# Out-projection weights split two tiles ahead, and eight low parts handed from VectorE to GpSimd, in a one-core decoder layer

## The chip, the cores and the metric

The kernel runs on one core of one Trainium2 chip. The metric is device time of one execution in microseconds; it is taken as the median over several executions. The profile is one further execution, recorded instruction by instruction.

## The reference, cut to what matters

One decoder layer over 1024 positions with width 1024 and a hidden width of 4096, all in float32:

```
h = x + concat[ sliding-window heads(RMSNorm(x)) | forgetting heads(RMSNorm(x)) ] @ W_o
y = h + relu( RMSNorm(h) @ W_u )**2 @ W_d
```

Eight heads use a banded softmax with sinks, eight use a causal softmax with a learned decay. The change touches the stretch in which `W_o` is multiplied, `h` is formed, and the factors for `W_u` are prepared.

## The kernel before, in words

Everything is kept with the features on the 128 partitions and the positions along the row. TensorE works on pairs of reduced-precision numbers: `split` (L73 to L80) casts a float32 tile to its high part on one engine, and then subtracts the high part from the tile on another engine, which gives the low part. Each product is three matmuls: high by high, high by low, low by high. A matmul of the line `mm` (L73) has 128x512 outputs in most stages.

**Attention.** The eight forgetting heads run two at a time. For each block of queries ScalarE makes the exponentials (`sb`, L689), VectorE scales them (L698), TensorE transposes them (`tpb`, L725), ScalarE casts the transposed tile (`pth`, L393), VectorE takes its low part (`ptl`, L394), and TensorE multiplies it with the values (`pvb`). The result of a head pair leaves by ScalarE and VectorE as `mtb` and `mix`, goes through a normalisation (`mixr`, `mixn`, `mixs`) out to a scratch tensor in memory `mixs_d` and comes back as the tile `mix6` (L850). In the gaps of these heads TensorE is given products of the out-projection.

**Out-projection.** The output has eight tiles `dt` of 128 features. `out_first` multiplies the first half of the contraction for all eight tiles and parks the sums, added to `x`, in the scratch tensor `part_d`. The second half is done by three functions. `out_weights(dt, 4)` loads 256 KB of `W_o` (`wor`, L857, two buffers), casts its high part on ScalarE (L77) and subtracts its low part on GpSimd (L80) into a tile `wos`, in the slots `w0` and `w1` by turns. `out_products` issues 24 matmuls. `out_finish` loads the parked sum (`h`, L956), adds the products on VectorE (L958), writes `h` to the scratch tensor `h_d` (L959), and makes the seven tiles `bh1` to `bh7` and their low parts `bl1` to `bl7` that the next stage multiplies: two or three are gained copies of `h`, made by `h_split` (L947 on ScalarE, L948 on VectorE), the others are sums `ts` (L965, L977), split by `sum_splits`. The tiles `dt` are finished in the order 0, 4, 1, 5, 2, 6, 3, 7. A pair (t, t + 4) fills the fourth `t` of every `bh` and `bl`; `ts` has one buffer, so that the sums of `t + 1` wait until all splits of `t` have read it.

Tiles 0 and 4 are begun inside the attention (`ahead_of`); the loop over 1, 5, 2, 6, 3, 7 makes weights, products and finish of one tile after the other.

**Up.** Seven products per column tile `j` of `W_u`, in the order 1, 2, 3, 6, 7, 5, 4, replace eight. `up(j)` builds sums of weights (`wus`, L1018, L1021), splits each weight tile `wu` (ScalarE casts, the low part is VectorE's for 2, 6, 5 and GpSimd's for the others), and issues 12 matmuls `pu` for each. The `wu` tiles rotate through the slots `w0` to `w6`, which the tiles `h` and `wos` had. Of `t` = 3, `bh5`, `bl5`, `bh4` and `bl4` are made after the product 2 of `j` = 0.

**What sets the order.** The engines run their instructions strictly in the order in which a scheduler wrote them down when the program was built. It works from the code's order, the data dependencies and its own costs; `issue_after` adds a dependency that only holds something back in that order. All loads and stores go through SyncE's queue, which is in order as well: a transfer that has to wait for a buffer holds up those behind it. GpSimd's and VectorE's work lies in their own queues in the same way.

Of the kernel before, what the change touches and what calls it, by code (L numbers as in the profile page):

```python
# [8 lines left out]
F32 = mybir.dt.float32  # L9
F32R = mybir.dt.float32r  # L10
BF16 = mybir.dt.bfloat16
AF = mybir.ActivationFunctionType
ALU = mybir.AluOpType
# [3 lines left out]
P = 128  # L17
# [38 lines left out]
def hybrid_layer(  # L56
# [13 lines left out]
    nc = tc.nc  # L70

    def mm(out, lhsT, rhs, start, stop):
        return nc.tensor.matmul(out, lhsT, rhs, start=start, stop=stop)  # L73

    def split(hi, lo, src, hi_eng, lo_eng):
        if hi_eng is nc.scalar:
            hi_eng.copy(hi, src)  # L77
        else:
            hi_eng.tensor_copy(hi, src)
        lo_eng.tensor_tensor(out=lo, in0=src, in1=hi.bitcast(F32), op=ALU.subtract)  # L80

    def rsqrt(pool, out, t, shape, tag):
        r0 = pool.tile(shape, F32, tag=tag + "r0", name="r0")
# [14 lines left out]
        out=ident, in_=ident, pattern=[[-1, P]], compare_op=ALU.not_equal,  # L98
# [17 lines left out]
    for i in range(2):  # L116
        nc.vector.tensor_tensor(
            out=gqk[:, i : i + 1], in0=vec[:, 2 * i : 2 * i + 1],
            in1=vec[:, 2 * i + 1 : 2 * i + 2], op=ALU.mult,
# [24 lines left out]
    def slot(tag, name, shape, dt=F32, pool=None):  # L144
        pool = o[pool or ("zw" if tag[0] == "w" else "zl")]
        return pool.tile([P] + shape, dt, tag=tag, name=name, bufs=1)
# [7 lines left out]
    def x_part(j, k, rows):  # L154

        c, r0 = divmod(rows.start, 512)
        return X[c][k // 2][:, j, k % 2, r0 : r0 + rows.stop - rows.start]
# [11 lines left out]
        out=maskd, in_=maskd, pattern=[[-1, P]], compare_op=ALU.is_ge,  # L169
# [6 lines left out]
    def w_tiles(n):  # L176


        w = wp.tile([P, 2 * WL], F32R, tag="w", name="w", bufs=8)
        wr = wp.tile([P, WN], F32, tag="wr", name="wr", bufs=3)  # L180
        lo = 384 if n == 384 else 400
        return wr[:, :n], w[:, :n], w[:, lo : lo + n]
# [10 lines left out]
    for k in range(KT):  # L193
        xr = ap2.tile([P, S], F32, tag="s", name="xr", bufs=NS)
        wr, wh, wl = w_tiles(384)
        if k == 0:
            nc.sync.dma_start(wr, w_a0[:, k, :])
            nc.scalar.preload_act_table_set("natural_log_exp_and_others")
        nc.sync.dma_start(xr[:, halves[0]], xT[k * P : (k + 1) * P, halves[0]])
        if k:  # L200
            nc.sync.dma_start(wr, w_a0[:, k, :])
        nc.sync.dma_start(xr[:, halves[1]], xT[k * P : (k + 1) * P, halves[1]])
        split(wh, wl, wr, nc.vector, nc.gpsimd if k else nc.vector)
        for cs in halves:
            hi, lo = (x_part(j, k, cs) for j in range(2))
            nc.scalar.activation(hi, xr[:, cs], AF.Copy, scale=ga[:, k : k + 1])
            last_x = nc.vector.scalar_tensor_tensor(  # L207
                out=lo, in0=xr[:, cs], scalar=ga[:, k : k + 1],
                in1=hi.bitcast(F32), op0=ALU.mult, op1=ALU.subtract,
            )  # L210
        passes = ((0, wh), (0, wl), (1, wh))
        order = (
            [(t, j) for j in range(3) for t in range(NT)] if k == 0
            else [(t, j) for t in (range(NT) if k < KT - 1 else LAST) for j in range(3)]
        )
        for t, j in order:
            part_, w_ = passes[j]
            mm(
                qps[t][:, :384], x_part(part_, k, slice(t * P, (t + 1) * P)), w_,
                k == 0 and j == 0, k == KT - 1 and j == 2,  # L220
            )
# [180 lines left out]
    for t in range(NT):  # L402
# [4 lines left out]
        out=rt, in0=rt, scalar1=1.0 / D, scalar2=EPS, op0=ALU.mult, op1=ALU.add  # L407
# [6 lines left out]
    for t in range(0, NT, 4):  # L414
# [8 lines left out]
        out=dist, in_=dist, pattern=[[-1, 256]], compare_op=ALU.is_ge, fill=BIG,  # L423
# [3 lines left out]
        out=dist, in_=dist, pattern=[[1, 256]], compare_op=ALU.is_ge, fill=BIG,  # L427
# [8 lines left out]
    for pattern, base, sign in (  # L436
# [5 lines left out]
            out=before, in_=before, pattern=pattern, compare_op=ALU.is_ge, fill=0.0,  # L442
# [407 lines left out]
        nc.sync.dma_start(mixt[e].bitcast(F32), mixs_d[e].rearrange("c p s -> p c s"))  # L850

    nout = [0]

    def out_weights(dt, e0):
        i = nout[0] = nout[0] + 1
        wr = o["zw"].tile([P, 4, P], F32, tag="wor", name="wor", bufs=2)
        nc.sync.dma_start(wr, w_o[dt][:, e0 : e0 + 4, :])  # L857
        w = slot(f"w{i % 2}", "wos", [2, 4, P], F32R)
        split(w[:, 0], w[:, 1], wr, nc.scalar, nc.gpsimd)
        return w[:, 0], w[:, 1]  # L860

    def out_products(ps, w, es):
        wh, wl = w
        for e in es:
            j = e % 4
            for c in range(2):
                cs = slice(c * 512, (c + 1) * 512)
                mm(ps[c], wh[:, j, :], mh[e][:, cs], j == 0, False)
                mm(ps[c], wh[:, j, :], ml[e][:, cs], False, False)
            for c in range(2):  # L870
                cs = slice(c * 512, (c + 1) * 512)
                mm(ps[c], wl[:, j, :], mh[e][:, cs], False, j == 3)

    def first_banks():
        return [o["pm0"].tile([P, 512], F32, tag=f"m{c}", name=f"po{c}") for c in range(2)]

    def out_first(dt):
        xt = slot(f"w{2 + dt % 2}", "xt", [S])
        nc.sync.dma_start(xt, xT[dt * P : (dt + 1) * P, :])
        w = out_weights(dt, 0)  # L880
        ps = first_banks()
        with paced():
            out_products(ps, w, range(4))
        t = slot("w4", "pc", [S])
        for c in range(2):
            cs = slice(c * 512, (c + 1) * 512)
            nc.scalar.copy(t[:, cs], ps[c])
            nc.gpsimd.tensor_tensor(out=xt[:, cs], in0=xt[:, cs], in1=t[:, cs], op=ALU.add)
        nc.sync.dma_start(part_d[dt], xt)
# [17 lines left out]
    for dt in (0, 4):  # L907
        ps = first_banks() if dt == 0 else [
            pa.tile([P, 512], F32, tag="sc", name=f"po{c}", bufs=2) for c in range(2)
        ]  # L910
        ahead_of.append((dt, ps, out_weights(dt, 4)))
# [25 lines left out]
    bh, bl = {}, {}  # L937
# [2 lines left out]
        bl[n] = slot(f"c{2 * i + 1}", f"bl{n}", [4, 512], F32R, "zr")  # L940
    rr = o["zr"].tile([P, S], F32, name="rr")
    left, right = slice(0, 512), slice(512, 1024)
    part = {}

    def h_split(n, t, src, gain):
        hi, lo = bh[n][:, t, :], bl[n][:, t, :]
# [5 lines left out]
    def out_finish(dt, ps):  # L952
        t, gain = dt % 4, gm[:, dt : dt + 1]
        h = slot(f"w{2 + dt // 4}", "h", [S]) if dt < 7 else rr
        with tc.issue_after(part["load"].ins) if dt == 7 else nullcontext():
            part["load"] = nc.sync.dma_start(h, part_d[dt])  # L956
        for c, cs in enumerate((left, right)):
            nc.vector.tensor_tensor(out=h[:, cs], in0=ps[c], in1=h[:, cs], op=ALU.add)  # L958
        nc.sync.dma_start(h_d[dt], h)  # L959
        if dt < 4:  # L960
            h_split(1, t, h[:, left], gain)
            ts = part["t"] = slot("m4", "ts", [4, 512])
            b12 = part["b12"] = slot("w4", "b12", [512])
            nc.scalar.activation(b12, h[:, right], AF.Copy, scale=gain)
            nc.vector.scalar_tensor_tensor(  # L965
                out=ts[:, 0], in0=h[:, left], scalar=gain, in1=b12, op0=ALU.mult, op1=ALU.subtract
            )
            return
        ts, b12 = part["t"], part["b12"]
        h_split(2, t, h[:, left], gain)  # L970
        h_split(3, t, h[:, right], gain)
        for i, q, other, op in (
            (1, right, ts[:, 0], ALU.add),
            (2, right, b12, ALU.subtract),
            (3, left, ts[:, 1], ALU.subtract),
        ):
            nc.vector.scalar_tensor_tensor(  # L977
                out=ts[:, i], in0=h[:, q], scalar=gain, in1=other, op0=ALU.mult, op1=op
            )
        part["rest"] = lambda: sum_splits(ts, t, ((0, 5), (3, 4)))  # L980
        sum_splits(ts, t, ((1, 6), (2, 7)))
        if t < 3:
            part.pop("rest")()

    def sum_splits(ts, t, which):
        for i, n in which:
            split(bh[n][:, t], bl[n][:, t], ts[:, i], nc.scalar, nc.vector)

    for dt, ps, w in ahead_of:
        out_finish(dt, ps)  # L990
    pda.close()
# [5 lines left out]
    def up_load(j):  # L997
        raws[j] = slot(f"r{j % 2}" if j else "m3", "wur", [2, KT, P])
        for i in range(2):
            up_loads[j] = nc.sync.dma_start(raws[j][:, i], w_u[j + i * NJ])  # L1000

    for dt in (1, 5, 2, 6, 3, 7):
        w = out_weights(dt, 4)
        ps = [bank(f"po{c}") for c in range(2)]
        out_products(ps, w, range(4, 8))
        out_finish(dt, ps)
        if dt == 2:
            with tc.issue_after(part["load"].ins):
                up_load(0)
# [267 lines left out]
    for i in range(len(STEPS)):  # L1277
        down(i)
        if STEPS[i][0] == len(PHASES) - 1 and late:
            name, dt, cs = late.pop(0)  # L1280
# [63 lines left out]
```

## Time and profile before

| | us |
|---|---|
| median of 3 executions | 1093.83 (1093.57 to 1095.04) |
| the profiled execution, by its own time | 1092.15 |
| its span | 1090.4 |
| TensorE busy in the span | 1078.7 (99%) |
| VectorE busy | 777.7 (71%) |
| ScalarE busy | 569.9 (52%) |
| GpSimd busy | 362.5 (33%) |

Times inside the profile run from the span's start. The attention's last heads run until about 436 us; the out-projection's last six tiles run on TensorE from 440.5 to 473.3; the first up products follow. A row of the timeline is: start, duration, engine, line, operation, output and inputs, shapes, how many in a row, and in brackets how long the engine had been idle and which instruction ended the wait. The durations of ScalarE's rows with x2 are of both together. SPq is SyncE's queue of transfers; the row of a transfer's issue says nothing of its landing, which the view of transfers gives.

### The profile page before, as it was taken

What the parts mean: (1) busy time and instruction counts of PE and PEld (TensorE: products, weight loads), DVE (VectorE), ACT (ScalarE), POOL (GpSimd) and SP (SyncE); (2) the same over time, 40 slices, a digit from 0 to 9 for tenths busy, and PEclk for the clock granted to TensorE, in tenths of its full rate; (3) what the DMA queues carried; (4) which work ended last, traced back from release to release, by engine and by line L of the source; (5) the groups of instructions that cost most, each with busy time, mean ns of one, the idle gap of its engine ahead of it and who ended that gap; (6) DMA issues with size and microseconds to landing.
All of it is one profiled execution on the core that took longest, in us unless ns stands there. A gap on an engine that the chain in (4) does not pass through costs nothing.

```text
span 1090.4 us, 15689 instructions
## 1 busy us (share of the span) xinstructions
PE 1078.7 (99%) x5557; PEld 933.5 (86%) x5557; DVE 777.7 (71%) x1327; ACT 569.9 (52%) x1013; POOL 362.5 (33%) x352
## 2 busy tenths in 40 slices
PE   9999999999999999999999999999999999999998
PEld 8999999999997888778888888888888888888886
DVE  7377677767765676998686869867675876674395
ACT  5558588666766756554545444353633433333331
POOL 5672523435434634333222232322222222231100
PEclk9999999999999999999999999999999999999999
DMA  9401212335656565663545543443998886665523
GB/s 308 141 27 48 72 37 61 115 87 154 209 192 221 167 223 174 212 231 126 198 179 179 189 153 135 149 170 145 333 390 311 299 289 227 241 228 181 174 87 116
DMA packets 96079, 195.69 MB, mean 179 GB/s; under 512 B 7376, under 2 KB 19584, under 8 KB 96000
## 3 DMA queue, kind: packets, MB, share of 16 engines
q1 hardware_dynamic: 95856, 194.66, 51.4%
q8 instruction: 44, 0.72, 0.3%
q14 instruction: 35, 0.29, 0.1%
q10 hardware_dynamic: 144, 0.02, 0.0%
HBM read 141.61 MB, written 53.04 MB: 179 GB/s over the span
## 4 chain that ended last, share of the span: by engine, by line
PE 82%; DMA 6%; DVE 6%; issue 2%; ACT 2%; POOL 1%; SPq 0%; ACTq 0%; POOLq 0%; DVEq 0%
PE pu L73 28%; PE pd L73 28%; PE ps L73 10%; PE po L73 5%; PE spb L73 3%; PE pvb L73 2%; PE tpb L725 2%; PE sp L73 1%; PE pv L73 1%; DMA wr<-in_w_b_dram 1%; DMA xq<-in_x_dram 1%; PE tpa L554 1%; DMA xr<-in_xT_dram 1%; DMA mixs_d<-mixn 1%; DVE x L207 1%
## 5 line engine op out<-in xcount | busy, mean ns | idle before, releaser
L73 PE MATMUL pd<-hx,wx 128*128 128x512 f32 (+1 forms) x1350 | 304.9, 388 | 0.0
L73 PEld LDWEIGHTS pd<-hx,wx 128*128 128x128 f32 x1350 | 252.7, 188 | 52.2
L73 PE MATMUL pu<-bh,wu 128*128 128x512 f32 x896 | 276.6, 390 | 1.0 <-ACT bh L947 1.0
L73 PE MATMUL ps<-w,x 128*128 128x384 f32 (+1 forms) x960 | 199.0, 345 | 0.4 <-DVE z L451 0.3
L73 PEld LDWEIGHTS pu<-bh,wu 128*128 128x128 f32 x896 | 168.1, 188 | 36.4 <-ACT bh L947 1.4
L73 PE MATMUL pu<-bl,wu 128*128 128x512 f32 x448 | 174.0, 389 | 0.0
L73 PEld LDWEIGHTS ps<-w,x 128*128 128x128 f32 x960 | 165.2, 189 | 3.7 <-DVE z L451 0.6
L77 ACT CAST hx<-hr 128x1024 fp32r<-128x1024 f32 x56 | 59.1, 1055 | 176.2 <-PE pd L73 171.2
L80 POOL TENSOR_TENSOR wx<-wda,wx 128x1024 fp32r<-128x1024 f32 x24 | 64.5, 2687 | 196.4 <-ACT wx L77 196.4
L80 DVE TENSOR_TENSOR hx<-hr,hx 128x1024 fp32r<-128x1024 f32 x56 | 72.2, 1297 | 71.0 <-ACT hx L77 71.0
L73 PEld LDWEIGHTS pu<-bl,wu 128*128 128x128 f32 x448 | 84.1, 188 | 17.7 <-issue 0.2
L73 PE MATMUL po<-mix,wos 128*128 128x512 f32 x384 | 94.8, 396 | 1.0 <-ACT wos L77 1.0
L73 PEld LDWEIGHTS po<-mix,wos 128*128 128x128 f32 x384 | 70.5, 188 | 15.5 <-ACT wos L77 1.5
L80 POOL TENSOR_TENSOR wu<-wus,wu 128x512 fp32r<-128x512 f32 x32 | 45.6, 1426 | 113.0 <-ACT wu L77 113.0
L80 POOL TENSOR_TENSOR wu<-wur,wu 128x512 fp32r<-128x512 f32 x32 | 44.2, 1380 | 102.5 <-ACT wu L77 102.5
L1018 DVE TENSOR_TENSOR ht<-hb 128x512 f32<-128x512 f32 x32 | 21.8, 723 | 62.8 <-ACT hb L1073 62.8
L394 DVE TENSOR_TENSOR ptl<-tpb,pth 128x512 fp32r<-128x512 f32 (+1 forms) x80 | 49.5, 631 | 21.9 <-ACT pth L393 18.9
L80 POOL TENSOR_TENSOR w<-wr,w 128x384 fp32r<-128x384 f32 (+1 forms) x47 | 51.5, 1106 | 40.1 <-ACT w L77 29.4
L77 ACT CAST wu<-wus 128x512 fp32r<-128x512 f32 x64 | 38.0, 618 | 48.3 <-PE pu L73 39.9
L77 ACT CAST wx<-wda 128x1024 fp32r<-128x1024 f32 x56 | 58.5, 1049 | 6.6 <-DMA wda<-in_w_d_dram 6.6
L689 ACT ACTIVATE sb<-sb,nmb 128x128 f32<-128x128 f32 (+3 forms) x64 | 49.8, 779 | 22.7 <-DVE nmb L683 22.6
L1072 ACT ACTIVATE hb<-hb 128x2048 f32<-128x2048 f32 x16 | 30.7, 1917 | 48.0 <-DVE hb L1021 47.9
(210 smaller groups left out, 1839.3 us busy)
## 6 DMA issues: line engine op xcount, KB each, us to landing
wda<-in_w_d_dram SPq DMA_DIRECT2D x34, 1024.0 KB, 9.2
hr<-hid_d SPq DMA_DIRECT2D x56, 512.0 KB, 5.7
wur<-in_w_u_dram SPq DMA_DIRECT2D x32, 512.0 KB, 4.3
hid_d<-ht SPq DMA_DIRECT2D x16, 1024.0 KB, 4.5
hid_d<-hb SPq DMA_DIRECT2D x16, 768.0 KB, 3.6
mix<-mixs_d SPq DMA_DIRECT2D x7, 1024.0 KB, 5.8
wr<-in_w_b_dram SPq DMA_DIRECT2D x32, 192.0 KB, 2.5
xr<-in_xT_dram SPq DMA_DIRECT2D x16, 256.0 KB, 5.0
```

Source lines behind the costliest of these rows:

```text
L73: return nc.tensor.matmul(out, lhsT, rhs, start=start, stop=stop)
L77: hi_eng.copy(hi, src)
L80: lo_eng.tensor_tensor(out=lo, in0=src, in1=hi.bitcast(F32), op=ALU.subtract)
L207: last_x = nc.vector.scalar_tensor_tensor(out=lo, in0=xr[:, cs], scalar=ga[:, k : k + 1], in1=hi.bitcast(F32), op0=ALU.mult, op1=ALU.subtract,
L394: nc.vector.tensor_tensor(out=lo[:, cols], in0=pt[:, cols], in1=hi[:, cols].bitcast(F32), op=ALU.subtract)
L554: nc.tensor.transpose(tp[:, hh * P : (hh + 1) * P], pts[hh // 2][:, hh % 2, c0 : c0 + P], ident)
L689: nc.scalar.activation(pr[:, :nk], pr[:, :nk], AF.Exp, scale=-1.0, bias=nm[:, c : c + 1], accum_out=dn_b[p % 2][:, h, i : i + 1] if p < 3 ...
L725: nc.tensor.transpose(tp[:, c0 : c0 + P], probs[qi][:, kb * P : (kb + 1) * P], ident)
L1018: eng.tensor_tensor(out=out, in0=a, in1=b, op=ALU.subtract)
L1072: nc.scalar.activation(b, b, AF.Relu)
```

## The change: what it does

Three things.

1. The weights of tiles 1 and 5 are made before the finishes of tiles 0 and 4 are written down. These two weight tiles go to the slots `w6` and `w5`.
2. In the loop, the weights of the tile two places on are made after a tile's products and before its finish.
3. The low parts `bl5` and `bl4` (eight instructions, two for each `t`) are GpSimd's and no longer VectorE's. `issue_after` places them behind the low part of the weights that were made last before.

```diff
@@ split
-        lo_eng.tensor_tensor(out=lo, in0=src, in1=hi.bitcast(F32), op=ALU.subtract)
+        return lo_eng.tensor_tensor(out=lo, in0=src, in1=hi.bitcast(F32), op=ALU.subtract)
@@ out_weights
-        w = slot(f"w{i % 2}", "wos", [2, 4, P], F32R)
-        split(w[:, 0], w[:, 1], wr, nc.scalar, nc.gpsimd)
+        w = slot(f"w{i % 2 + (5 if i in (11, 12) else 0)}", "wos", [2, 4, P], F32R)
+        part["weights"] = split(w[:, 0], w[:, 1], wr, nc.scalar, nc.gpsimd)
@@ sum_splits
         for i, n in which:
-            split(bh[n][:, t], bl[n][:, t], ts[:, i], nc.scalar, nc.vector)
+            last = n in (5, 4)
+            with tc.issue_after(part["weights"].ins) if last else nullcontext():
+                split(
+                    bh[n][:, t], bl[n][:, t], ts[:, i], nc.scalar,
+                    nc.gpsimd if last else nc.vector,
+                )
+    rest = (1, 5, 2, 6, 3, 7)
+    ws = [out_weights(dt, 4) for dt in rest[:2]]
     for dt, ps, w in ahead_of:
         out_finish(dt, ps)
...
-    for dt in (1, 5, 2, 6, 3, 7):
-        w = out_weights(dt, 4)
+    for i, dt in enumerate(rest):
         ps = [bank(f"po{c}") for c in range(2)]
-        out_products(ps, w, range(4, 8))
+        out_products(ps, ws[i], range(4, 8))
+        if i + 2 < len(rest):
+            ws.append(out_weights(rest[i + 2], 4))
         out_finish(dt, ps)
```

What this makes of the engines' orders is shown at two places. The numbers behind the names tell tiles apart. The first place is ScalarE's order in the last part of the attention, from the cast of `mixn_5210` on, which is the row of 412.78 us in the timeline before. `wos_5606` belongs to tile 4. Before:

```order
L77 CAST mixn_5210<-mixr_5209 128x512
L689 ACTIVATE sb_5462,dnb_5464<-sb_5462,nmb_5463 128x256
L887 COPY pc_5445<-po0_5419 128x512
L887 COPY pc_5445<-po1_5420 128x512
L77 CAST wos_5606<-wor_5604 128x512
L393 CAST pth_5391<-tpb_5387 128x384
L393 CAST pth_5478<-tpb_5473 128x512
L689 ACTIVATE sb_5505,dnb_5507<-sb_5505,nmb_5506 128x640
L393 CAST pth_5490<-tpb_5486 128x384
L741 COPY mtb_5401<-pvb_2494 64x256
L393 CAST pth_5540<-tpb_5535 128x512
L689 ACTIVATE sb_5520,dnb_5522<-sb_5520,nmb_5521 128x768
```

After; `wos_5744` belongs to tile 1 and `wos_5749` to tile 5:

```order
L77 CAST mixn_5210<-mixr_5209 128x512
L77 CAST wos_5744<-wor_5742 128x512
L689 ACTIVATE sb_5462,dnb_5464<-sb_5462,nmb_5463 128x256
L889 COPY pc_5445<-po0_5419 128x512
L889 COPY pc_5445<-po1_5420 128x512
L77 CAST wos_5606<-wor_5604 128x512
L393 CAST pth_5391<-tpb_5387 128x384
L393 CAST pth_5478<-tpb_5473 128x512
L77 CAST wos_5749<-wor_5747 128x512
L689 ACTIVATE sb_5505,dnb_5507<-sb_5505,nmb_5506 128x640
L393 CAST pth_5490<-tpb_5486 128x384
L689 ACTIVATE sb_5520,dnb_5522<-sb_5520,nmb_5521 128x768
```

The casts of the weights of tiles 1 and 5 now stand inside the softmax of the last heads, each ahead of an exponential. Before, both stood behind the attention, as the row of 439.85 us. SyncE still loads these two tiles here, but the second load (`wor_5747`) is now queued behind the first tile's low part on GpSimd.

The second place is GpSimd's order from the last of the attention's work to the first weights of the up stage. In the rows before, the first two are tiles 1 and 5, then 2, 6, 3 and 7 follow, and `wu_6063` and `wu_6103` are the weights of the up products 1 and 3:

```order
L80 TENSOR_TENSOR wos_5780<-wor_5778,wos_5780 128x512
L80 TENSOR_TENSOR wos_5822<-wor_5820,wos_5822 128x512
L80 TENSOR_TENSOR wos_5873<-wor_5871,wos_5873 128x512
L80 TENSOR_TENSOR wos_5918<-wor_5916,wos_5918 128x512
L80 TENSOR_TENSOR wu_6063<-wur_5913,wu_6063 128x512
L80 TENSOR_TENSOR wos_5969<-wor_5967,wos_5969 128x512
L80 TENSOR_TENSOR wos_6011<-wor_6009,wos_6011 128x512
L80 TENSOR_TENSOR wu_6103<-wus_6058,wu_6103 128x512
```

After; the first two are tiles 2 and 6, and `wos_5909` and `wos_5954` are tiles 3 and 7:

```order
L80 TENSOR_TENSOR wos_5816<-wor_5814,wos_5816 128x512
L80 TENSOR_TENSOR wos_5858<-wor_5856,wos_5858 128x512
L80 TENSOR_TENSOR bl5_5738<-ts_5759,bh5_5737 128x512
L80 TENSOR_TENSOR bl4_5740<-ts_5759,bh4_5739 128x512
L80 TENSOR_TENSOR bl5_5738<-ts_5826,bh5_5737 128x512
L80 TENSOR_TENSOR wu_6063<-wur_5923,wu_6063 128x512
L80 TENSOR_TENSOR bl4_5740<-ts_5826,bh4_5739 128x512
L80 TENSOR_TENSOR wos_5909<-wor_5907,wos_5909 128x512
L80 TENSOR_TENSOR wos_5954<-wor_5952,wos_5954 128x512
L80 TENSOR_TENSOR bl5_5738<-ts_5919,bh5_5737 128x512
L80 TENSOR_TENSOR bl4_5740<-ts_5919,bh4_5739 128x512
L80 TENSOR_TENSOR wu_6103<-wus_6058,wu_6103 128x512
```

Behind the weights of tiles 2 and 6 there now stand four rows, one of them a `wu`, before the weights of tile 3.

More of the change, by code (lines that the diff above doesn't have):

```diff
@@ L852, in hybrid_layer @@
     nout = [0]
+    part = {}
     def out_weights(dt, e0):
@@ L942, in hybrid_layer @@
     left, right = slice(0, 512), slice(512, 1024)
-    part = {}
     def h_split(n, t, src, gain):
```

## The prediction

> **What bounds the kernel now.** I read the page first (busy time, costliest groups), then the waits of TensorE from 410 to 500 us, then the busy time by stage, and then the timelines of the single engines around the places that the change touches. Page, and the view of waits:
>
> ```profile
> PE 1078.7 (99%) x5557; PEld 933.5 (86%) x5557; DVE 777.7 (71%) x1327; ACT 569.9 (52%) x1013; POOL 362.5 (33%) x352
> ...
> PE pu L73 <- ACT bh L947: 1.0, 1, 1.0
> PE po L73 <- ACT wos L77: 0.7, 1, 0.7
> PE tpb L725 <- DVE ptl L394: 0.5, 1, 0.5
> ```
>
> TensorE is the bound, and no work of its own is removed. In the stretch of the change it waits three times, for 2.2 us. The windows (length, then busy time and instructions of each engine) show how close the others are:
>
> ```profile
> 400.00:436.00 36.00, 35.39 (x225) 30.39 (x224) 25.99 (x63) 22.78 (x50) 14.23 (x23) 1.00 0.55 185
> 436.00:474.00 38.00, 37.31 (x165) 30.57 (x164) 35.72 (x51) 20.84 (x35) 9.71 (x7) 1.00 0.66 214
> 474.00:500.00 26.00, 25.03 (x111) 20.42 (x110) 26.00 (x36) 12.72 (x22) 11.99 (x7) 1.00 0.39 152
> ```
>
> TensorE's idle time here is 0.61 + 0.69 + 0.97 = 2.3 us. This is all that earlier weights or a relieved VectorE can bring; what they can cost has no such ceiling. From 436 us on VectorE is busy 94% and then 100%, GpSimd 26% and 46%. TensorE's timeline at the places that matter:
>
> ```profile
> 419.58 3.00 PE L73 MATMUL po<-mix,wos 128*128 128x512 f32 x12
> 422.42 1.03 PE L725 MATMUL tpb<-ident,sb 128*128 128x128 f32 x8
> 425.27 1.26 PE L725 MATMUL tpb<-ident,sb 128*128 128x128 f32 x7 [0.53 <-DVE ptl L394]
> 431.25 3.02 PE L73 MATMUL po<-mix,wos 128*128 128x512 f32 x12
> 440.50 32.93 PE L73 MATMUL po<-mix,wos 128*128 128x512 f32 x144 [0.69 <-ACT wos L77]
> 477.12 0.73 PE L73 MATMUL pu<-bh,wu 128*128 128x512 f32 x2 [0.97 <-ACT bh L947]
> ```
>
> 144 matmuls in 32.93 us are 0.229 us each; one tile (24) is 5.49 us.
>
> **The change part by part. (a) The gap at 440.50.** With the weights of tile 1 there, TensorE need not wait for them: −0.69. VectorE's add of tile 0 or 4, which frees a bank, is the next to be late:
>
> ```profile
> 439.40 0.69 DVE L958 TENSOR_TENSOR h<-po,h 128x512 f32<-128x512 f32 x1 [0.21 <-PE po L73]
> ```
>
> It ends at 440.09, so the gain lies between −0.4 (440.50 − 440.09, if every product of tile 1 waits for it) and −0.69; I take −0.6, since the first products go to the other bank.
>
> **(b) The two casts inside the softmax.** ScalarE, one GpSimd row, transfers (a row of issue, and below it the view of transfers with the KB and the us from issue to landing) and one VectorE row:
>
> ```profile
> 412.78 0.62 ACT L77 CAST mixn<-mixr 128x512 fp32r<-128x512 f32 x1 [0.19 <-DVE mixr L613]
> 413.72 0.51 ACT L689 ACTIVATE sb<-sb,nmb 128x256 f32<-128x256 f32 x1 [0.32 <-DVE nmb L683]
> 415.37 1.07 ACT L887 COPY pc<-po 128x512 f32<-128x512 f32 x2 [1.04 <-PE po L73]
> 416.85 0.98 ACT L393 CAST pth<-tpb 128x384 fp32r<-128x384 f32 x2
> 418.24 0.83 ACT L689 ACTIVATE sb<-sb,nmb 128x640 f32<-128x640 f32 x1 [0.40 <-DVE nmb L683]
> 422.56 0.62 ACT L77 CAST mixn<-mixr 128x512 fp32r<-128x512 f32 x1
> 439.85 1.13 ACT L77 CAST wos<-wor 128x512 fp32r<-128x512 f32 x2
> ...
> 464.23 1.31 POOL L80 TENSOR_TENSOR wos<-wor,wos 128x512 fp32r<-128x512 f32 x1 [1.60 <-ACT wos L77]
> ...
> 411.68 0.33 SPq L857 DMA_DIRECT2D wor<-in_w_o_dram  x1
> wor<-in_w_o_dram SPq DMA_DIRECT2D x1, 256.0 KB, 3.0
> 414.81 0.32 SPq L616 DMA_DIRECT2D mixs_d<-mixs  x1
> mixs_d<-mixs SPq DMA_DIRECT2D x1, 256.0 KB, 5.2
> ...
> 419.52 1.22 DVE L698 TENSOR_SCALAR sb<-sb,dnb 128x640 f32<-128x640 f32 x1
> ...
> 427.57 0.37 SPq L850 DMA_DIRECT2D mix<-mixs_d  x1
> mix<-mixs_d SPq DMA_DIRECT2D x1, 1024.0 KB, 5.0
> ```
>
> The load issued at 411.68 lands 3.0 us later, at 414.7. ScalarE is free at 413.40 and must now cast these weights first: the cast (0.6, half of 1.13) ends at 415.3 and the exponential of 256 begins 1.6 late. That alone is covered: ScalarE then waited 1.04 for TensorE's `po` anyhow, so the two `pc` end near 416.95 and not 416.44, the cast of tile 4's weights and the two `pth` near 418.5. There stands the second cast. Its load sits on SyncE behind GpSimd's low part of the first (1.3 us): cast until 415.3, low part until 416.6, issue at 416.65, landing 3.0 later at 419.65 or, behind the 256 KB that landed at 414.81 + 5.2 = 420.0, about 0.7 after that, 420.7 (`mix`, with 768 KB more, takes 2.0 longer than `wor`: 0.7 for 256 KB). After a cast of 0.6 the exponential of 640 starts at 420.3 to 421.3 and not at 418.24: 2.0 to 3.1 late.
>
> What of this reaches TensorE? The scaled tile of 640 was there 1.7 before its use at 422.42 (419.52 + 1.22 = 420.74), so 0.3 to 1.4 pass at once. Then nothing is slack: the next transposes already wait 0.53 for `ptl`, and the tile `mix6` came with no margin. It landed at 427.57 + 5.0 = 432.57; its first product is the seventh of the twelve from 431.25, at 432.62. Its chain begins with the cast `mixn` at 422.56, which stands behind the late exponentials, and with one more `pth` (0.5) ahead of it. On GpSimd the first low part also goes ahead of the scaling of the tile of 256, the two `xt` and the zeroing of `pth`. Ends: 0.3 (only what passes at once) and 4.7 (the 3.1, the second cast 0.6, the `pth` 0.5, and 0.5 of the loop's wait again). I take 3.6, near the upper end, because of the two rows without slack. What hides none of it: later stages are TensorE-bound, so lost time isn't won back.
>
> **(c) GpSimd's queue.** GpSimd and VectorE, same stretch:
>
> ```profile
> 459.63 1.30 POOL L80 TENSOR_TENSOR wu<-wur,wu 128x512 fp32r<-128x512 f32 x1 [4.88 <-ACT wu L77]
> 461.19 1.44 POOL L80 TENSOR_TENSOR wos<-wor,wos 128x512 fp32r<-128x512 f32 x1 [0.27 <-ACT wos L77]
> 449.26 1.30 POOL L80 TENSOR_TENSOR wos<-wor,wos 128x512 fp32r<-128x512 f32 x1 [5.66 <-ACT wos L77]
> 464.30 1.78 DVE L948 SCALAR_TENSOR_TENSOR bl<-h,vt,bh 128x512 fp32r<-128x512 f32 x1
> 469.07 0.67 DVE L80 TENSOR_TENSOR bl<-ts,bh 128x512 fp32r<-128x512 f32 x1
> 449.30 1.28 DVE L958 TENSOR_TENSOR h<-po,h 128x512 f32<-128x512 f32 x2
> ```
>
> Tile 3 is the fifth of six: TensorE reaches it at 440.50 + 96 × 0.229 = 462.5, and its low weights with the fifth matmul, at 463.4. Their low part ended at 462.63: a margin of 0.7. Now a `bl4` of 1.3 stands between `wu` and this tile, so it comes 0.6 late; if the `bl5` ahead of `wu` is late too, 1.9. On the other hand TensorE arrives later by (a) and (b), and `wu` hangs on loads, not on TensorE: then nothing is lost. Between 0 and 1.9, I take 1.0.
>
> **(d) VectorE against GpSimd.** An L948 that begins 0.07 after a GpSimd subtraction lasts 1.78, and ends 0.54 after it (466.08 against 465.54), where 0.73 is usual: one GpSimd row costs a busy VectorE about 1.05. Adds from TensorE's banks are not stretched (the L958 pair of 1.28 lies beside the GpSimd row at 449.26). Moving eight rows of 0.67 saves VectorE 5.4 us and can cost it 8 × 1.05 = 8.4: a net loss of up to 3.0 over the stretch in which it's nearly always busy, and a gain of 5.4 where the rows meet only adds. [...]
>
> Who waits for VectorE there? The `bh1` of t = 3, through ScalarE:
>
> ```profile
> 475.83 0.62 ACT L77 CAST wu<-wus 128x512 fp32r<-128x512 f32 x1 [2.12 <-DMA h_d<-h]
> 476.35 0.72 ACT L947 ACTIVATE bh<-h,vt 128x512 fp32r<-128x512 f32 x1
> 469.19 0.37 SPq L959 DMA_DIRECT2D h_d<-h  x1
> h_d<-h SPq DMA_DIRECT2D x1, 512.0 KB, 6.6
> ```
>
> A weight cast waits for the slot that the store of `h` leaves (469.19 + 6.6 = 475.8), and `bh1`, queued behind it, costs TensorE 0.97. The store follows VectorE's adds. Ends: −0.97 (VectorE a little earlier, two `wor` loads out of the queue) and +2.1 (two more meetings on the way). I take +0.9. The rest of up's first column, where VectorE is at 100%, feels the same meetings through `bl3` and `bl6` of t = 3: between 0 and 1.7, I take 0.7. The moved `bl4` of t = 3 itself is needed by the last product and lies behind the weights there; I cost it nothing.
>
> **Sum:** −0.6 + 3.6 + 1.0 + 0.9 + 0.7 = +5.6. Against the profiled execution 1092.15 + 5.6 = 1097.7; that execution lies 1.7 under the median, so the median after is 1093.83 + 5.6 = 1099.4. A fifth of a per cent, 2.2 us, is what a measurement of this kernel tells from no change.
>
> **The rivals.**
> 1. *Covered softmax* (about the same). The exponential of 640 is late, but the loop behind it absorbs all but 0.4, and GpSimd's queue is covered by the shift: −0.6 + 0.4 + 0 + 0.9 + 0.3 = +1.0, 1094.8. For it: ScalarE idles 0.40 and 1.04 in this loop, and the 1.7 of slack at 422.42. Against it: the `ptl` wait and `mix6`.
> 2. *Faster.* VectorE's relief decides: the GpSimd rows fall on adds from the banks, `h` is added and stored sooner, `bh1` is no longer late, and the softmax absorbs everything. All of TensorE's idle time goes, −2.3, 1091.5. It decides from the point where the exponential of 640 starts less than 1.7 late and the store of 469.19 goes out 1 us sooner. For it: VectorE's 94% and 100%. Against it: the landing of the second load at 419.65 or later, which makes the exponential 2.0 late, and that TensorE would have to wait for nothing at all.
> 3. *GpSimd's queue as the main loss.* `bl5` and `bl4` wait for ScalarE's `bh` casts, and weights of tile 3 or 7 behind them come late by two rows each: +1.9 and +1.3 in place of 1.0, the rest as forecast: +7.8, 1101.6.
>
> **How the numbers follow.** Forecast with its neighbours (b from 2 to 4.7, the others within their ends): 0.55, its own range 1096.2 to 1101.5. Rival 3: 0.17. Rival 1: 0.20, of which a fifth lies beyond +2.2. Rival 2: 0.08, of which 0.03 stay within 0.2%. Slower by over 0.2%: 0.55 + 0.17 + 0.04 = 0.76; same: 0.16 + 0.03 = 0.19; faster: 0.05. The range, 1093 to 1102.5, leaves out rival 2, the lower edge of rival 1, and the tops of (b), (c) and (d) together.
>
> **What the profile after would show.** Right: the timeline of ScalarE has a weight cast waiting for `wor` ahead of the exponential of 640, which starts after 420; TensorE waits for `ptl` or `pth` between 422 and 430, and perhaps for `mix`; no wait for `wos` at the first of the six tiles, but one for GpSimd's `wos` at tile 3; a wait for `bh` L947 (now L948) above 0.97; VectorE's L977 and L948 rows of 1.8 more often than before. Wrong: the exponential of 640 before 419.5, or waits of TensorE from 410 to 500 us that sum to less than 2.2.

## The result: 0.5% slower, in three places

The changed kernel takes 1101.27 us in the median of 7 executions (1098.74 to 1102.78), the kernel before 1094.67 beside it (1093.57 to 1097.29). The ratio is 1.0051, 95% interval 1.0038 to 1.0064: about +5.6 us, which is the size that was forecast. (The two medians lie 6.6 apart, and 1101.27 is 1.9 above the forecast time.) The profiled execution took 1099.15, its span is 1097.4 and not 1090.4.

The part ahead of the change starts up to 6 us earlier or later from execution to execution (the 60th last transposition `tpb`, L725, starts between 396.0 and 401.9 us in the profiles of this study; the three latest, 398.5 to 401.9, are the three in which the granted clock fell to 0.62 for some 4.5 us between 337 and 345 us, and the rest of the spread isn't explained), and everything from the 85th up product on takes 596.9 us in all of them but one (597.1). So single profiles are compared by three stages between, worked out from the starts of four instructions of TensorE: that transposition, the first product of tile 1 (the 144th last `po`), the first up product `pu`, and the 85th (a column has 84). There is one profile of each kernel, so a stage has no interval; the ratios of the times have one.

| us | start | to tile 1 | to the first `pu` | first column | sum |
|---|---|---|---|---|---|
| before | 395.95 | 44.55 | 32.77 | 20.31 | 97.63 |
| changed | 396.12 | 46.43 | 35.00 | 23.03 | 104.45 |
| change | | +1.88 | +2.23 | +2.72 | +6.8 |

The view of TensorE's waits in the changed kernel, 405 to 510 us, and the windows:

```profile
PE pu L73 <- ACT bh L948: 2.0, 1, 2.0
PE tpb L725 <- DVE ptl L394: 1.9, 3, 0.9
PE po L73 <- POOL wos L80: 1.5, 1, 1.5
PE tpb L725 <- DVE dnb L696: 0.5, 1, 0.5
PE po L73 <- DMA mix<-mixs_d: 0.3, 1, 0.3
```

```profile
400.00:436.00 36.00, 33.24 (x208) 27.91 (x207) 26.72 (x63) 23.44 (x51) 16.20 (x25) 1.00 0.60 201
436.00:474.00 38.00, 36.45 (x165) 29.47 (x164) 31.41 (x40) 16.18 (x28) 13.40 (x9) 1.00 0.49 166
474.00:500.00 26.00, 23.95 (x99) 19.28 (x98) 23.50 (x32) 13.54 (x23) 12.84 (x8) 0.93 0.56 202
```

Three waits of 2.2 us have become seven of 6.2. VectorE's busy time fell from 35.72 to 31.41 in the second window, but GpSimd's rose by 3.7 and TensorE's fell: VectorE has less work there, and it also waits, as the third place below shows. And in the last window the granted clock is 0.93. TensorE's rows:

```profile
423.72 0.63 PE L725 MATMUL tpb<-ident,sb 128*128 128x128 f32 x4 [0.54 <-DVE dnb L696]
424.95 0.55 PE L725 MATMUL tpb<-ident,sb 128*128 128x128 f32 x3 [0.61 <-DVE ptl L394]
427.35 0.55 PE L725 MATMUL tpb<-ident,sb 128*128 128x128 f32 x3 [0.86 <-DVE ptl L394]
428.36 0.66 PE L725 MATMUL tpb<-ident,sb 128*128 128x128 f32 x4 [0.46 <-DVE ptl L394]
435.52 1.65 PE L73 MATMUL po<-mix,wos 128*128 128x512 f32 x6 [0.26 <-DMA mix<-mixs_d]
467.43 10.28 PE L73 MATMUL po<-mix,wos 128*128 128x512 f32 x44 [1.46 <-POOL wos L80]
482.02 0.50 PE L73 MATMUL pu<-bh,wu 128*128 128x512 f32 x1 [2.04 <-ACT bh L948]
482.64 1.05 PE L73 MATMUL pu<-bh,wu 128*128 128x512 f32 x2
486.02 0.63 PE L73 MATMUL pu<-bh,wu 128*128 128x512 f32 x2
```

The first five rows are the softmax and `mix6`; the gap at tile 1 has gone. Behind the wait for `bh1`, two matmuls take 1.05, where a pair takes 0.61 or 0.62 in the kernel before, and 0.63 again from 486.02: between 482.6 and 485.6 eight matmuls start 0.43 apart (the last 0.39) and not 0.23, which costs 8 × 0.2 = 1.6.

**First place: the softmax.** ScalarE in the changed kernel:

```profile
414.62 0.62 ACT L77 CAST wos<-wor 128x512 fp32r<-128x512 f32 x1 [1.06 <-DMA wor<-in_w_o_dram]
419.85 0.62 ACT L77 CAST wos<-wor 128x512 fp32r<-128x512 f32 x1 [1.76 <-DMA wor<-in_w_o_dram]
420.37 0.83 ACT L689 ACTIVATE sb<-sb,nmb 128x640 f32<-128x640 f32 x1
426.47 0.62 ACT L77 CAST mixn<-mixr 128x512 fp32r<-128x512 f32 x1
```

Both early casts wait for their loads with the exponentials queued behind them. The exponential of 640 starts at 420.37 (418.24 before), the cast `mixn` at 426.47 (422.56).

**Second place: tile 3's low weights.** GpSimd:

```profile
462.71 1.30 POOL L80 TENSOR_TENSOR wu<-wur,wu 128x512 fp32r<-128x512 f32 x1 [5.87 <-ACT wu L77]
464.28 1.43 POOL L80 TENSOR_TENSOR bl<-ts,bh 128x512 fp32r<-128x512 f32 x1 [0.26 <-DMA h_d<-h]
465.67 1.70 POOL L80 TENSOR_TENSOR wos<-wor,wos 128x512 fp32r<-128x512 f32 x1
```

The weights wait behind `wu` and `bl4`, end at 467.37, and TensorE goes on at 467.43.

**Third place: the first up column.** Here the order on VectorE counts. Before, the adds of tile 2 (L958) stand among the first work on the up weights:

```profile
458.12 1.29 DVE L80 TENSOR_TENSOR bl<-ts,bh 128x512 fp32r<-128x512 f32 x2
459.33 0.69 DVE L958 TENSOR_TENSOR h<-po,h 128x512 f32<-128x512 f32 x1
460.10 1.37 DVE L80 TENSOR_TENSOR wu<-wur,wu 128x512 fp32r<-128x512 f32 x1
461.39 0.68 DVE L958 TENSOR_TENSOR h<-po,h 128x512 f32<-128x512 f32 x1
```

Changed, they stand behind all of it:

```profile
459.97 0.68 DVE L80 TENSOR_TENSOR bl<-ts,bh 128x512 fp32r<-128x512 f32 x1
463.19 1.37 DVE L80 TENSOR_TENSOR bl<-ts,bh 128x512 fp32r<-128x512 f32 x1 [2.54 <-ACT bh L77]
464.48 1.78 DVE L1032 TENSOR_TENSOR wus<-wur 128x512 f32<-128x512 f32 x1
466.18 1.74 DVE L1029 TENSOR_TENSOR wus<-wur 128x512 f32<-128x512 f32 x1
467.85 0.68 DVE L80 TENSOR_TENSOR wu<-wur,wu 128x512 fp32r<-128x512 f32 x1
468.45 1.28 DVE L959 TENSOR_TENSOR h<-po,h 128x512 f32<-128x512 f32 x2
```

Counted from tile 1's first product, tile 2's first add starts 18.8 us on before (459.33 − 440.50), and 25.9 us on now (468.45 − 442.55). The 2.54 us that VectorE waits at 463.19 come from ScalarE, where the cast of `bh` stands behind a cast of `wu` that waits for the load of the up weights:

```profile
462.02 0.62 ACT L77 CAST wu<-wur 128x512 fp32r<-128x512 f32 x1 [3.96 <-DMA wur<-in_w_u_dram]
462.54 0.62 ACT L77 CAST bh<-ts 128x512 fp32r<-128x512 f32 x1
```

VectorE's own three rows of up weights then take 4.0 (464.48 to 468.45). Every later add, store of `h` and `bh` follows; the last of that chain is the `bh1` that TensorE waits for.

### The profile page after: what moved, and what is told of

Read it like the earlier page. It is cut to its first block, busy times and chain, and to the rows that moved or that the text cites. A ratio compares the mean times of both kernels' runs of the same rounds, so it can differ in the third digit from the quotient of the medians.

```text
span 1097.4 us, 15691 instructions
## 1 busy us (share of the span) xinstructions
PE 1082.1 (99%) x5557; PEld 934.6 (85%) x5557; DVE 767.9 (70%) x1319; ACT 571.0 (52%) x1013; POOL 375.9 (34%) x360
## 4 chain that ended last, share of the span: by engine, by line
PE 56%; DVE 2%; DMA 2%; issue 0%; ACT 0%; SPq 0%; ACTq 0%; DVEq 0%
PE pu L73 28%; PE pd L73 27%; DMA h_d<-h 1%; PE po L73 0%; DMA wur<-in_w_u_dram 0%; DVE h L959 0%; DMA mix<-mixs_d 0%; PE pvb L73 0%; DVE ts L966 0%; DVE wus L1029 0%; DVE m L1032 0%; DVE pd L1272 0%; DVE bl L949 0%; DMA wor<-in_w_o_dram 0%; DVE bl L80 0%
## 5 line engine op out<-in xcount | busy, mean ns | idle before, releaser
L80 POOL TENSOR_TENSOR wu<-wus,wu 128x512 fp32r<-128x512 f32 x32 | 47.9, 1497 | 115.5 <-ACT wu L77 115.5
L393 ACT CAST pth<-tpb 128x512 fp32r<-128x512 f32 (+1 forms) x80 | 41.8, 542 | 18.3 <-PE tpb L725 13.1
```

What stands on the lines that cost most here:

```text
L80: return lo_eng.tensor_tensor(out=lo, in0=src, in1=hi.bitcast(F32), op=ALU.subtract)
L393: nc.scalar.copy(hi[:, cols], pt[:, cols])
```

## The experiments

Theory A, from the prediction: four separate places (softmax, gap at tile 1, GpSimd's queue, `bh1`). Rival R: VectorE held up by GpSimd's low parts (in the kernel before, an L948 of 1.78 beside a GpSimd row, where 0.73 is usual) is the loss as a whole. The stages of each run are in the table behind the last experiment.

**Each half alone.** The weights early, all low parts on VectorE:

```diff
-            last = n in (5, 4)
+            last = False
```

> The changed kernel with all low parts back on VectorE; only the weights come early. Theory A (four separate places: the softmax held by weight casts +3.2, the gap at the first tile -0.7, GpSimd's queue at tile 3 +1.5, the wait for bh1 and the slow clock behind it +2.8): the softmax loss and the removed gap stay, GpSimd's queue is free again, and bh1 is about as before: +2 to +4 us against the kernel before, TensorE's wait for GpSimd's wos gone. Rival R (VectorE blocked by GpSimd's low parts is the loss; a late softmax only moves waits): -0.7 to +1 us.

Measured: ratio 1.0044 (1.0031 to 1.0057). The softmax loss is there (46.85), the wait for GpSimd's `wos` isn't (32.81). But the first column is as late as with the whole change, 22.61, by two waits of TensorE in place of one, and the ratio is +4.8 us where theory A gave +2 to +4. The wait for `bh1` itself is as before (1.00), as theory A said, but the column is late all the same: this loss doesn't need GpSimd's low parts. Tile 2's first add starts 23.4 us behind tile 1 in this profile. TensorE's timeline of this kernel:

```profile
481.41 0.73 PE L73 MATMUL pu<-bh,wu 128*128 128x512 f32 x2 [1.00 <-ACT bh L948]
493.10 0.50 PE L73 MATMUL pu<-bl,wu 128*128 128x512 f32 x1 [1.04 <-DVE bl L80]
```

The low parts on GpSimd, the weights where they were before:

```diff
-    ws = [out_weights(dt, 4) for dt in rest[:2]]
...
+        w = out_weights(dt, 4)
...
-            ws.append(out_weights(rest[i + 2], 4))
```

> The kernel before with only bl5 and bl4 given to GpSimd; weights are made where they were. Theory A: the softmax as before (no wait for ptl above 0.6 us between 410 and 430), the 0.7 gap at the first of the six tiles stays, and GpSimd's queue and bh1 cost +1 to +4 us together. Rival R: +5 us or more, about all of the change's loss.

Measured: ratio 1.0035 (1.0023 to 1.0047). The softmax is undisturbed but for 0.4 at `mix6`, tile 3's wait is 1.52 (stage 34.63), the first column loses 1.4, and tile 2's first add starts 23.2 us behind tile 1. Rival R, which put nearly all here and nothing in the other half, falls; the two halves, +4.6 and +3.8 by their stages, overlap in the first column, where together they cost 2.7 and not 2.3 + 1.4.

**The casts out of the softmax.** ScalarE's two casts are ordered behind the copy of the last head but one:

```diff
-        part["weights"] = split(w[:, 0], w[:, 1], wr, nc.scalar, nc.gpsimd)
+        with tc.issue_after(left_by[-2]) if i in (11, 12) else nullcontext():
+            part["weights"] = split(w[:, 0], w[:, 1], wr, nc.scalar, nc.gpsimd)
```

> The changed kernel, but the two early weight casts are ordered on ScalarE behind the copy of the last head but one, out of the softmax. Theory A: the exponential of 640 starts near 418.2 again, TensorE's waits between 410 and 436 us fall to about 0.5, the gap at the first tile stays closed, and the total falls by about 3.2 us against the changed kernel: +2 to +4.5 against the kernel before. Rival R: no lower than +5.

Measured: ratio 1.0033 (1.0021 to 1.0045). The waits of TensorE from 405 to 520 us in this kernel:

```profile
PE pu L73 <- ACT bh L950: 2.0, 1, 2.0
PE po L73 <- POOL wos L80: 1.5, 1, 1.5
PE tpb L725 <- DVE ptl L394: 0.5, 1, 0.5
```

The softmax waits are back to the one of 0.5, and the gap at tile 1 stays closed: the first stage takes 43.55, 2.88 less than in the changed kernel and 1.00 less than before. The other two stages stay as they were (34.98, 22.99). So the two casts' places alone make the first loss, and early weights by themselves are worth 1 us in this stage.

**`bh1` ahead of the weights' cast.** In the changed kernel, the cast of product 5's weights, which waits for the store of `h`, goes behind `bh1` of `t` = 3:

```diff
-            split(w[:, 0], w[:, 1], src[n], nc.scalar, nc.vector if n in (2, 6, 5) else nc.gpsimd)
+            with tc.issue_after(part[1, 3].ins) if j == 0 and n == 5 else nullcontext():
+                split(w[:, 0], w[:, 1], src[n], nc.scalar, nc.vector if n in (2, 6, 5) else nc.gpsimd)
```

> The changed kernel, but the weight cast of product 5 (first column) is ordered on ScalarE behind bh1 of t = 3, and so bh1 no longer waits for the store of h. Theory A: the wait of 2.0 for bh1 shrinks to under 1 and the stretch of 0.43 us per matmul behind it goes with it, if a long wait is what lowers the clock: 2 to 3.5 us less than the changed kernel, +3 to +4.6 against the kernel before. Rival (the granted clock falls for a reason of its own): about 1 us less, and the slow matmuls are still there.

Measured: ratio 1.0058 (1.0046 to 1.007), no gain at all. TensorE's timeline of this kernel:

```profile
482.42 0.50 PE L73 MATMUL pu<-bh,wu 128*128 128x512 f32 x1 [1.15 <-ACT bh L948]
489.07 0.50 PE L73 MATMUL pu<-bl,wu 128*128 128x512 f32 x1 [0.45 <-DVE bl L949]
493.97 0.74 PE L73 MATMUL pu<-bh,wu 128*128 128x512 f32 x2 [1.40 <-POOL wu L80]
```

The wait for `bh1` fell to 1.15 (under 1 was forecast) and the slow matmuls went with it, as forecast (the granted clock is 1.00 from 474 to 500 us). But the first column still takes 22.96: what was won came back as 0.45 for `bl` and 1.40 for GpSimd's `wu`. So the place where TensorE waits isn't the cause; the work that leads up to it is late. This led to theory C: tile 2's adds stand on VectorE behind work that waits for the up weights' load.

**Tile 2's adds first.** VectorE's first two sums and the split of product 2's weights go behind these adds; in the changed kernel, the splits of products 1 and 2 also go behind ScalarE's cast `bh7` of `t` = 1:

```diff
-        plus(s[:, 0], a21, a22)
+        with tc.issue_after(part["add", 2].ins) if j == 0 else nullcontext():
+            plus(s[:, 0], a21, a22)
+            minus(s[:, 2], a11, a21)
...
+            held = {2: [part["add", 2], part["cast", 7, 1]], 1: [part["cast", 7, 1]]}.get(n, []) if j == 0 else []
```

In the changed kernel:

> The changed kernel whole, but on VectorE the sums and the low part of the first up weights stand behind the adds of tile 2, and on ScalarE the casts of these weights behind bh7 of t = 1. Theory C: the wait of 2.0 for bh1 falls under 1.2 and the slow matmuls behind it go: third stage 20.5 to 21.5 and not 23.0, 1.5 to 2.5 us less than the changed kernel; the softmax loss stays (46.4), the wait for GpSimd's wos at tile 3 stays above 0.8. [...]

Measured: ratio 1.0039 (1.0024 to 1.0054). VectorE and then TensorE in this kernel:

```profile
463.02 1.28 DVE L82 TENSOR_TENSOR bl<-ts,bh 128x512 fp32r<-128x512 f32 x2
464.22 1.28 DVE L961 TENSOR_TENSOR h<-po,h 128x512 f32<-128x512 f32 x2
466.41 0.90 DVE L1035 TENSOR_TENSOR wus<-wur 128x512 f32<-128x512 f32 x1 [0.90 <-DMA wur<-in_w_u_dram]
```

```profile
470.19 10.27 PE L73 MATMUL po<-mix,wos 128*128 128x512 f32 x44 [1.55 <-POOL wos L82]
493.05 0.73 PE L73 MATMUL pu<-bh,wu 128*128 128x512 f32 x2 [1.26 <-POOL wu L82]
```

The adds now start 18.6 us behind tile 1 (464.22 − 445.60). The wait for `bh1` and the slow matmuls are gone (the granted clock is 1.00 from 474 to 500 us), and the first column takes 20.60 in place of 23.03; the other two stages keep their losses (46.56, 34.69). A wait of 1.26 for GpSimd's `wu` remains. Theory C's range for the column is met. The times don't settle how much that is worth: 1.0039 lies below the changed kernel's 1.0051, but the intervals overlap. And the edit takes both queues at once, ScalarE's wait and VectorE's own rows, so the share of each isn't told apart.

With the casts held and all low parts on VectorE (and nothing ordered behind `bh7`):

> Early weights with their casts held behind the softmax, all low parts on VectorE, and VectorE's sums and low part of the first up weights ordered behind the adds of tile 2. Stage lengths before: 44.6 (to the first product of tile 1), 32.8 (to the first up product), 20.3 (84 up products); changed kernel: 46.4, 35.0, 23.0. Theory C (the first column is late because tile 2's adds stand on VectorE behind work that waits for the load of the up weights): 43.6, 32.8, 20.3 to 21.0, in sum 0 to -1 us against the kernel before. [...]

Measured: ratio 1.0008 (0.9997 to 1.0019), inconclusive against the kernel before; by the stages 44.24, 32.91, 21.29. The column is 1.3 faster than with the same low parts and the changed order (22.61), but still 1.0 slower than before, with waits of 0.41 for `bh` and 0.81 for VectorE's `bl`. It misses theory C's range (20.3 to 21.0) by 0.3. What causes that last microsecond wasn't found.

**Is the wait for `bh1` worth anything by itself?** With both, and in the kernel before:

> As the kernel with held casts, VectorE's low parts and tile 2's adds first, and in addition the weight cast of product 5 behind bh1 of t = 3 on ScalarE. If the wait for bh1 is a loss of its own: third stage 19.4, in sum -1 to -2 us against the kernel before. If, as in the changed kernel with that edit, VectorE's late work only shows up as another wait: third stage 20.3 or more, in sum 0 to -1.

> The kernel before with only that cast of product 5 behind bh1 of t = 3. If the wait of 0.97 for bh1 is a loss of its own: third stage 19.4, -1 us. If the first column is held by VectorE as a whole: 20.3, the wait appears at a later product, 0 us.

Measured: 1.0003 (0.999 to 1.0017) and 1.0008 (0.9994 to 1.0022), no difference that can be told from none. By the stages the first has its waits at `bl` now (21.71), and the second a column shorter by 0.58 (19.73) in its profile, which its times don't bear out.

**GpSimd's queue.** Both mends with all eight low parts on GpSimd, with those of `t` = 2 and 3 alone, and the latter with `bh1` first:

```diff
-            last = n in (5, 4)
+            last = n in (5, 4) and t >= 2
```

> The whole change with both mends: the early weight casts held behind the softmax, and tile 2's adds (and bh7 of t = 1) ahead of the first up weights. All eight low parts stay with GpSimd. If the three losses are separate: stages 43.6, 34.7 (the wait for GpSimd's wos at tile 3 stays, 1.5), 20.6 = 98.9 against 97.6 before: +1.2 us.

> As the kernel with both mends, but GpSimd has bl5 and bl4 only for t = 2 and 3 (four instructions), none ahead of tile 3's weights. If GpSimd's queue makes the wait at tile 3: it goes, stages 43.6, 32.9, 20.6 = 97.1: -0.5 us against the kernel before, and 1.5 less than with all eight. If the wait at tile 3 has another cause (the load, ScalarE's cast): 34 or more remains.

> As the kernel before this in the list, and the weight cast of product 5 behind bh1 of t = 3. Third stage 19.7 to 20.6, in sum 96.1 to 97.1: -0.5 to -1.5 us against the kernel before; more than that isn't possible, since TensorE idles only 2.3 us in this stretch.

Measured: 1.0027 (1.0016 to 1.0038), 1.0017 (1.0006 to 1.0028) and 1.0005 (0.9993 to 1.0018). The second stage is 34.25 with all eight and 32.85 with the four late ones: the wait at tile 3 is made by GpSimd's queue, and not by the load or ScalarE's cast. But what was won there came back in the column, which went from 21.26 to 22.37. The two stages together took 55.51 and 55.22; they take 53.08 in the kernel before, 58.03 in the changed one, and 54.20 with held casts, tile 2's adds first and all low parts on VectorE. So the losses of the second and third stage don't add up as separate ones. The forecasts for the sums missed (98.9, 97.1 and 96.1 to 97.1 against 99.99, 99.99 and 99.51). TensorE in the kernel with four:

```profile
436.22 1.65 PE L73 MATMUL po<-mix,wos 128*128 128x512 f32 x6 [0.92 <-DMA mix<-mixs_d]
491.05 0.74 PE L73 MATMUL pu<-bh,wu 128*128 128x512 f32 x2 [1.42 <-POOL wu L82]
```

`mix6`, the tile without margin, was 0.6 to 0.9 late in these three, and GpSimd's `wu` cost 1.2 to 1.4 in each. No version beats the kernel before.

| us | to tile 1 | to the first `pu` | first column | sum |
|---|---|---|---|---|
| weights only | 46.85 | 32.81 | 22.61 | 102.27 |
| low parts only | 45.10 | 34.63 | 21.75 | 101.47 |
| casts held | 43.55 | 34.98 | 22.99 | 101.53 |
| changed, `bh1` first | 46.74 | 34.68 | 22.96 | 104.38 |
| changed, adds first | 46.56 | 34.69 | 20.60 | 101.85 |
| held, VectorE, adds first | 44.24 | 32.91 | 21.29 | 98.43 |
| the same and `bh1` first | 43.57 | 32.85 | 21.71 | 98.13 |
| before, `bh1` first | 44.42 | 32.77 | 19.73 | 96.91 |
| held, adds first, all eight | 44.47 | 34.25 | 21.26 | 99.99 |
| the same, four late ones | 44.77 | 32.85 | 22.37 | 99.99 |
| the same and `bh1` first | 44.76 | 32.81 | 21.94 | 99.51 |

## Why the prediction was right, and where it wasn't

The sum, +5.6, is what the ratio gives. The profile, one execution, shows +6.8 for the same stretch, and against it the first two terms together are 1.1 too high, the third is 1.2 too low and the last two together are 1.1 too low. So the places were right, and the sum is in part luck. That the three places together make nearly all of the loss is shown: with the casts held, tile 2's adds first and all low parts on VectorE the ratio is 1.0008 (0.9997 to 1.0019). Term by term:

- **(a) and (b), the gap and the softmax: −0.6 + 3.6 forecast, +1.88 in the profile.** The mechanism is shown: the second load was issued at 416.64 (416.65 forecast) and landed by 419.85, the exponential of 640 started at 420.37 (420.3 to 421.3 forecast), and holding the casts took 2.9 off. That is (b), and what is left, 1.00 less than before, is (a). A gap costs more than its idle time here: around the wait of 1.46 at 467.43, two steps from one start to the next took 2.20 (465.57 to 467.77) where two of 0.23 are usual, 1.74 lost. So (a) was 0.4 too small, and the softmax absorbed 0.7 more than I allowed with "nothing is slack".
- **(c), GpSimd's queue: 1.0 forecast, 2.2 in the profile**, of which the one wait, with the slow steps around it, makes 1.74. The wait comes from the queue, as the runs with eight and four low parts show; but ending it won only 0.3 over the two stages, since the column took the rest back. The hope that TensorE's own lateness would cover half of it failed, since the load of `wur` shifted with TensorE (456.64, 14.1 us behind tile 1's start, against 13.4 before).
- **(d), VectorE: 0.9 + 0.7 forecast, 2.7 in the profile, and this is the step that failed in its reason.** I put it down to VectorE's meetings with GpSimd on the way to the store of `h`. The meetings are there: from tile 1's first product to the column's end, VectorE has twelve instructions of over 1 us in place of nine, and is busy for 52.75 us of 58.03 where it was 51.99 of 53.08, so the relief is gone. (The rows of 1.7 to 1.8 on L978 and L949 are not more often than on L977 and L948 before, two each, against the sign that I gave.) But the run with all low parts on VectorE lost nearly as much (22.61), and putting tile 2's adds ahead took the column from 23.03 to 20.60 with GpSimd's eight rows in place. The larger part is where the scheduler put those adds and, on ScalarE, the casts ahead of them; the orders of these two engines would have shown it. And the price of a wait was taken to be its length; behind 2.0 us the slow matmuls added 1.6.
- **"The moved `bl4` of t = 3 … I cost it nothing"** holds for that instruction. But with the `t` = 3 low parts on GpSimd, a `wu` of the first column is 1.2 to 1.4 late in six of the kernels, five of them with tile 2's adds or `bh1` mended. The `wu` of 3.1 ahead of it isn't new: it starts at 482.03 in the kernel before and lasts 3.10, and there too GpSimd had been idle for 2.5 ahead of it. What makes the product's low part late wasn't found.

Rival 3, GpSimd's queue as the main loss, is a third of the loss by the stages and not the most. Rival 2, faster, was right in one thing: with the casts held the first stage is 1.0 shorter than before. It then had nothing to gain elsewhere. VectorE's relief is in the second window, 4.3 us less busy; but tile 2's adds came 7 us later, since VectorE first waited for a cast behind a load and then worked on the up weights.

## What to carry to other kernels

Work that is moved ahead of a bound engine's last wait also moves, in every in-order queue that it passes, ahead of something else; read for each queue what now stands behind an instruction that waits for a load, above all on engines that are far from busy. When a mended wait comes back at the next consumer with the same sum, the wait isn't the cause: follow the chain back to the first instruction that starts later counted from a fixed point. With little idle time on the bound engine (2.3 us here; by the 1.74 for a wait of 1.46, some 3 us is an estimate of what ending all three waits could win) there is a ceiling on the gain and none such on the loss.

## What the hardware showed that I had not expected

Two waits of TensorE cost nearly twice their length, 3.6 us for 2.0. In the two profiles with a wait of 2.0 us (2.04 in the changed kernel, 2.01 with the casts held), eight of the next ten matmuls of 128x512 started about 0.43 apart and not 0.23, over 3.4 us (482.64 to 486.02, and 480.88 to 484.28), and the granted clock from the end of the wait to the last slow step was 0.57 (482.02 to 486.02, and 480.30 to 484.28); behind the waits of 0.4 to 1.55 us in this stretch none did (the granted clock is 1.00 in all other windows from 400 to 500 us).

The length of one wait doesn't decide it, though. Earlier in the attention, between 337 and 345 us, the granted clock was 0.62 over 4.5 us in three profiles, behind two shorter waits close together: 0.77 and 0.67 us (four late low parts), 0.81 and 1.45 (changed, adds first), 1.29 and 0.87 (held, VectorE, adds first). The kernel before has 0.77 and 0.64 at the same place and kept 1.00. What decides isn't shown by these runs.

The tile without margin varies: `mix6` made TensorE wait between 0 and 0.9 us in the six kernels with held casts, whose softmax waits are the same; why isn't known.
